# Key and value compression ahead of the query projections in the fill of the second block

## Chip, cores and metric

The kernel runs on one core of a Trainium2 chip. The metric is the device time of one execution in microseconds; the time before is the median of three runs. TensorE multiplies matrices and writes its results to PSUM; VectorE, ScalarE and GpSimd work on tiles in PSUM (not GpSimd) and SBUF; SP's queue issues most of the loads from device memory.

## What is computed

Two blocks over 512 tokens of width 1024, in 32-bit floats. The first block (two attentions, a gated merge, 32 experts of which four are used by each token) is not touched. The second block projects its input into 17 parts and feeds three mixers: a sparse attention (NSA, six heads in two groups), a stick-breaking attention (four heads) and a gated recurrence (HGRN, six heads). Their outputs are gated, projected and normalised. What the change touches belongs to the sparse attention:

```python
def compress(src, w1, w2):                     # for kc and vc
    blocks = src.reshape(B, S, G, dk)[:, blk_idx] + cmp_pos[None, None, :, None, :]
    blocks = blocks.transpose(0, 3, 1, 2, 4).reshape(B, G, n_cmp, CMP_BLOCK * dk)
    return jax.nn.gelu(blocks @ w1) @ w2

kc = compress(kc_src, w_ck1, w_ck2)
vc = compress(vc_src, w_cv1, w_cv2)
...
s_c = jnp.einsum('bghtd,bgnd->bghtn', qb, kc) * scale + bias_c
```

There are 31 overlapping blocks of 32 tokens; `w1` is 2048 x 128 and `w2` is 128 x 64. The scores of the queries against the compressed keys need both the compression and the query projections, and are computed well after either.

## The kernel before

The second block keeps its input transposed in SBUF, split into a high and a low half (`xTh`, `xTl`), so that a product in full precision is three matmuls: high by high, high by low, low by high (L132 to L134). A projection of 128 columns takes one chunk of weights (1024 x 128) and 24 matmuls, eight groups of three.

Weight chunks are loaded and split in the order of a list that `block2_plan` (L1191) writes; each chunk that is taken (`ws_get`, L211) writes the load of the second chunk after it and the split of the next one. A chunk is loaded by SP into `raw`, ScalarE copies the high half (L144) and VectorE subtracts it for the low half (L146). The chunks of the compression are kept as one tile of both halves (`whl`), those of the projections as two (`whi`, `wlo`). Buffers come from two pools: `S` with 17 large buffers (2048 elements per partition), `H` with 10 small ones (1024). A `raw`, a `whi` and a `wlo` of a 128-column chunk take a small one each, a `whl` a large one.

The order of the second block's work is written by hand. The recurrence (`hgrn`, L1609) runs in 66 steps, three head pairs through an input stage, a tree of six levels and an output stage. Beside it runs a fill: a chain of generators that give out matmuls piece by piece. `mix_in` (L64) takes 160 pieces of fill for 72 steps of the recurrence, and what is left of the fill behind them. The fill is the forget and query projections of the recurrence (`P_fq`, 32 pieces for the two that belong to the fill) and the parts that the string `F1` names, in its order:

- `s`, `P_stick` (L1324), 48 pieces: queries, keys and values of the stick-breaking attention
- `v`, `P_v` (L1344), 32: values, gates and two key projections of the sparse attention
- `p`, `P_blocks` (L1367), 16: the sources of the compression, laid out in overlapping blocks (`Y`)
- `b`, `block2_bias` (L1239), 1: the position biases, twelve matmuls (L1251), written to device memory and read back (`t5d`, `tz`)
- `q`, `P_nq` (L1436), 24: the three query projections; each result is split by ScalarE (L144) and VectorE (L148)
- `c`, `P_compress` (L1385), 16: for the key and then the value, sixteen matmuls of `Y` with the chunks of `w_ck1` or `w_cv1` (L1406), then the halves are summed by four matmuls (L1414), then gelu in small steps on VectorE and ScalarE (L1415 to L1421), then the product with `w2` (L1425 or L1431) and the layout of the result (L1427 to L1433); the key's result is split into `kc`

Behind the fill come the gated projections of the recurrence's output (`P_zh`, L1456) woven with the start of the stick-breaking attention, then that attention, the sparse attention (`nsa`, L1678) and the remaining gates, then the output projection.

The order of writing is a priority, not the order of the queues: at compile time a planner puts the instructions of each engine into its queue, and pulls later work ahead where earlier work isn't ready or has no buffer. On the chip each queue then runs in the order that was fixed.

Of the kernel before, what the change touches and what calls it, by code (L numbers as in the profile page):

```python
# [38 lines left out]
FI = -1  # L39
RP = 1  # L40
HP = 50
F1, F2, F3 = "svpbqc", "h", "z"
WS, WN, WZ = 34, 78, 50
NA, NB = 66, 38
ZO = 3, 0, 1, 4, 2
# [43 lines left out]
class K:  # L89
# [1101 lines left out]
    def block2_plan(self):  # L1191
        w, a = self.a["w_in_2"], self.a
        c0 = 0
        for n in [512] + [128] * 10 + [256, 128, 18] + [128] * 7 + ["w_ck1_2", "w_cv1_2"] + [128] * 8:
            if isinstance(n, str):
                for x in range(2):
                    self.ws_add([128, 8, 128], (lambda r: r, a[n][1024 * x:1024 * x + 1024].rearrange("(k p) c -> p k c", p=128)),
                                joint=True)
            else:
                if n == 512:  # L1200
                    self.ws_wide(w, c0)
                else:
                    self.ws_cols(w, c0, n)
                c0 += n
        w3 = a["w_out_2"].rearrange("(k p) c -> p k c", p=128)
        for x in (1, 0):
            for n in range(2):
                self.ws_add([128, 4, 512], (lambda r: r, w3[:, 4 * x:4 * x + 4, 512 * n:512 * n + 512]))
# [740 lines left out]
```

## Time and profile before

| | us |
|---|---|
| median of three runs | 2056.35 |
| lowest, highest run | 2055.72, 2062.5 |
| the profiled execution | 2060.52 |
| its span in the trace | 2058.7 |

The span runs from the first to the last instruction of the program; 1.8 us of the profiled execution lie around it. The second block's part that matters lies between 1690 and 1860 us of the span: the recurrence with its fill up to about 1848, then the gated projections and the attentions. In the rows below, an engine's busy time in a stretch is to be held against the stretch's length, and "idle before" in brackets is the time for which an engine stood still ahead of an instruction, with what ended it.

### The profile page before, as it was taken

The numbers are of one execution on the slowest core, as the hardware profiler recorded it, in microseconds if no ns is written. First come the engines' busy times: TensorE is split into PE (matmuls) and PEld (weight loads), VectorE is DVE, ScalarE is ACT, GpSimd is POOL, SyncE is SP. The second block draws the span as 40 slices with busy tenths as digits, with TensorE's granted clock in tenths as the row PEclk, the third lists the DMA queues.
The fourth block names the chain that finished last, engine by engine and source line by source line (L and its number), as shares of the span: only waits on it lengthen the run. The fifth ranks groups of instructions, "written<-read, shape, count | busy, mean of one in ns | idle before, by whom it ended". The sixth has DMA issues, their size and how long they took to land. (4 is left out here: it accounts for less than half of the span.)

```text
span 2058.7 us, 26167 instructions
## 1 busy us (share of the span) xinstructions
PE 1971.5 (96%) x9926; PEld 1592.3 (77%) x9926; DVE 1641.5 (80%) x2095; ACT 1242.7 (60%) x1342; POOL 353.8 (17%) x225
## 2 busy tenths in 40 slices
PE   5999999999999999999999799899998899999997
PEld 4777778878888888888888688688886678867765
DVE  5574444689999999999999798799998868557676
ACT  4564443347776768677776576676866456346651
POOL 3000000121223222222222222222221000010000
PEclk9999999999999999999999899999999999999998
DMA  6151214569999999999999799899998532141121
GB/s 196 53 169 44 72 61 145 208 251 341 374 365 368 377 376 373 375 370 377 364 382 367 296 371 356 312 373 369 380 372 325 214 101 71 35 131 42 58 105 41
DMA packets 162708, 512.71 MB, mean 249 GB/s; under 512 B 19913, under 2 KB 94953, under 8 KB 113424
## 3 DMA queue, kind: packets, MB, share of 16 engines
q1 hardware_dynamic: 139104, 466.80, 61.4%
q0 software_dynamic: 14448, 29.03, 3.9%
q10 hardware_dynamic: 9024, 15.16, 2.1%
q8 instruction: 79, 1.29, 0.2%
q14 instruction: 53, 0.43, 0.1%
HBM read 505.51 MB, written 28.97 MB: 260 GB/s over the span
## 5 line engine op out<-in xcount | busy, mean ns | idle before, releaser
L146 DVE TENSOR_TENSOR wlo<-raw,whi 128x2048 fp32r<-128x2048 f32 (+1 forms) x466 | 978.8, 2130 | 116.0 <-ACT whi L144 74.7
L144 ACT ACTIVATE whi<-raw 128x2048 fp32r<-128x2048 f32 (+1 forms) x466 | 819.6, 1792 | 193.3 <-PE sc L134 78.4
L133 PE MATMUL mm<-wlo,xT 128*128 128x512 f32 x1024 | 401.1, 392 | 8.8 <-DVE wlo L146 8.8
L134 PE MATMUL mm<-whi,xT 128*128 128x512 f32 x1024 | 405.6, 396 | 0.0
L132 PE MATMUL mm<-whi,xT 128*128 128x512 f32 x1024 | 360.0, 400 | 5.2 <-ACT whi L144 5.2
L959 POOL DMA_INDIRECT accd<-h,sx x30 | 158.1, 5271 | 466.4 <-DVE h L958 447.9
L133 PEld LDWEIGHTS mm<-wlo,xT 128*128 128x128 f32 x1024 | 193.6, 189 | 47.5 <-DVE wlo L146 9.8
L132 PEld LDWEIGHTS mm<-whi,xT 128*128 128x128 f32 x1024 | 193.7, 189 | 42.2 <-ACT whi L144 5.8
L134 PEld LDWEIGHTS mm<-whi,xT 128*128 128x128 f32 x1024 | 193.0, 188 | 39.4
L133 PE MATMUL sc<-wlo,xT 128*128 128x512 f32 x512 | 201.3, 393 | 0.0
L134 PE MATMUL sc<-whi,xT 128*128 128x512 f32 x512 | 200.6, 392 | 0.0
L132 PE MATMUL sc<-whi,xT 128*128 128x512 f32 x512 | 183.0, 391 | 0.0
L144 ACT ACTIVATE xT<-tp 128x512 fp32r<-128x512 f32 x126 | 74.9, 594 | 175.8 <-PE tp L898 174.1
L133 PEld LDWEIGHTS sc<-wlo,xT 128*128 128x128 f32 x512 | 96.8, 189 | 21.3 <-DVE wlo L146 0.6
L134 PEld LDWEIGHTS sc<-whi,xT 128*128 128x128 f32 x512 | 96.7, 189 | 20.6
L132 PEld LDWEIGHTS sc<-whi,xT 128*128 128x128 f32 x512 | 96.6, 189 | 20.3
L132 PE MATMUL mm<-hTh,whi 128*128 128x512 f32 x256 | 106.6, 416 | 0.3 <-ACT whi L144 0.3
L1167 ACT ACTIVATE p<-s,mn 128x128 f32<-128x128 f32 (+3 forms) x112 | 62.2, 557 | 73.2 <-DVE mn L1163 69.4
L1163 DVE CUSTOM_DVE_ANT_0 s<-sc,bias 128x256 f32<-128x256 f32 (+3 forms) x99 | 45.6, 482 | 74.2 <-PE sc L140 64.4
L874 POOL DMA_INDIRECT xg<-h1d,sx x31 | 74.0, 2386 | 168.6 <-PE mm L134 90.7
L134 PE MATMUL mm<-hTh,wlo 128*128 128x512 f32 x256 | 100.6, 393 | 0.6 <-DVE wlo L146 0.6
L133 PE MATMUL mm<-hTl,whi 128*128 128x512 f32 x256 | 100.8, 394 | 0.0
(463 smaller groups left out, 3091.4 us busy)
## 6 DMA issues: line engine op xcount, KB each, us to landing
raw<-in_w_exp_in_dram SPq DMA_DIRECT2D x256, 1024.0 KB, 7.4
raw<-in_w_exp_out_dram SPq DMA_DIRECT2D x128, 1024.0 KB, 7.3
raw<-in_w_in_dram SPq DMA_DIRECT2D x58, 512.0 KB, 3.9
raw<-in_w_out_dram SPq DMA_DIRECT2D x8, 1024.0 KB, 5.9
raw<-in_w_in_dram SPq DMA_DIRECT2D x7, 1024.0 KB, 8.4
x<-in_x_dram SPq DMA_DIRECT2D x4, 512.0 KB, 6.8
hd<-h SPq DMA_DIRECT2D x4, 512.0 KB, 2.6
raw<-in_w_branch_a_dram SPq DMA_DIRECT2D x4, 512.0 KB, 3.4
```

Of the source, the lines that this page charges most:

```text
L132: mm(out, lh, rh, start=start, stop=False, **kw)
L133: mm(out, lh, rl, start=False, stop=False, **kw)
L134: return mm(out, ll, rh, start=False, stop=stop, **kw)
L144: h = nc.scalar.activation(hi, src, AF.Copy, scale=scale)
L146: l = (eng or nc.vector).tensor_tensor(lo, src, f(hi), op=OP.subtract)
L874: self.nc.gpsimd.indirect_dma_start(out=dst, out_offset=None, in_=src[:, :], in_offset=bass.IndirectOffsetOnAxis(ap=ix[:, 0:1], axis=0), b ...
L959: nc.gpsimd.indirect_dma_start(out=self.accd[:, :], out_offset=bass.IndirectOffsetOnAxis(ap=ix[:, 0:1], axis=0), in_=y, in_offset=None, bo ...
L1163: nc.vector.tensor_tensor_reduce(s[:, :kl], sc[:, :kl], bias, op0=OP.add, op1=OP.min, scale=1.0, scalar=3e38, accum_out=mn)
L1167: nc.scalar.activation(p[:, :kl], s[:, :kl], AF.Exp, scale=-1.0, bias=mn, accum_out=sm)
```

## The change

The string `F1` names the compression ahead of the query projections, and the list of weight chunks puts the four chunks of the compression (two of `w_ck1`, two of `w_cv1`) ahead of the three of the queries, so that the list still agrees with the order in which chunks are taken. No instruction is added or removed.

```diff
-F1, F2, F3 = "svpbqc", "h", "z"
+F1, F2, F3 = "svpbcq", "h", "z"
...
     def block2_plan(self):
         w, a = self.a["w_in_2"], self.a
         c0 = 0
-        for n in [512] + [128] * 10 + [256, 128, 18] + [128] * 7 + ["w_ck1_2", "w_cv1_2"] + [128] * 8:
+        for n in [512] + [128] * 10 + [256, 128, 18] + [128] * 4 + ["w_ck1_2", "w_cv1_2"] + [128] * 11:
             if isinstance(n, str):
```

## Rows read from the trace of the kernel before

**Rows 1.** The profile's page, its first part: busy time, share of the span, instructions.

```profile
span 2058.7 us, 26167 instructions
...
PE 1971.5 (96%) x9926; PEld 1592.3 (77%) x9926; DVE 1641.5 (80%) x2095; ACT 1242.7 (60%) x1342; POOL 353.8 (17%) x225
```

**Rows 2.** Table by stretch: length, busy (instructions) per engine, clock, DMA share, GB/s.

```profile
1805.00:1830.50 25.50, 25.50 (x117) 18.41 (x116) 13.70 (x27) 13.27 (x21) 8.16 (x24) 1.00 0.58 176
1830.50:1842.70 12.20, 7.68 (x48) 7.03 (x47) 8.16 (x18) 5.27 (x8) 0.00 (x0) 0.72 0.58 144
1842.70:1860.00 17.30, 17.30 (x76) 11.98 (x75) 8.84 (x21) 10.51 (x17) 0.00 (x0) 1.00 0.11 30
1860.00:1900.00 40.00, 40.00 (x278) 31.95 (x276) 30.22 (x77) 20.54 (x37) 0.00 (x0) 1.00 0.15 41
1900.00:2020.00 120.00, 117.39 (x772) 82.25 (x772) 77.75 (x255) 68.67 (x158) 1.40 (x3) 1.00 0.21 70
```

**Rows 3.** Timeline of TensorE around the compression: start, us, line, tiles, idle before.

```profile
1829.68 0.39 PE L134 MATMUL mm<-xTh,wlo 128*128 128x512 f32 x1
...
1830.36 0.39 PE L134 MATMUL mm<-xTh,wlo 128*128 128x512 f32 x1
1830.59 2.08 PE L1406 MATMUL sc<-whl,Y 128*128 128x256 f32 x16
...
1835.62 0.43 PE L1425 MATMUL sc<-cw 128*128 128x64 f32 x2 [1.39 <-DVE cw L1421]
1839.16 3.75 PE L1406 MATMUL sc<-whl,Y 128*128 128x256 f32 x16 [3.10 <-DVE whl L146]
1842.74 0.40 PE L132 MATMUL mm<-xTh,whi 128*128 128x512 f32 x1
```

**Rows 4.** Timeline of ScalarE, same columns: splits of the compression's weights.

```profile
1821.25 1.05 ACT L144 ACTIVATE whl<-raw 128x1024 fp32r<-128x1024 f32 x1
...
1836.65 0.26 ACT L144 ACTIVATE kc<-cw 128x64 fp32r<-128x64 f32 x1 [1.56 <-DVE cw L1427]
1836.81 1.99 ACT L144 ACTIVATE whl<-raw 128x1024 fp32r<-128x1024 f32 x2
```

**Rows 5.** Table by stretch, finer, for the granted clock.

```profile
1835.60:1839.10 3.50, 0.43 (x2) 0.30 (x2) 1.82 (x5) 2.45 (x4) 0.00 (x0) 0.55 0.29 73
1839.10:1842.70 3.60, 3.54 (x16) 3.54 (x17) 3.41 (x4) 1.59 (x2) 0.00 (x0) 0.50 0.02 5
```

**Rows 6.** Timeline of SP's queue, 1800 to 1830: start, us, line, loads.

```profile
1805.10 8.76 SPq L194 DMA_DIRECT2D raw<-in_w_ck_dram  x2
1819.76 1.29 SPq L1712 DMA_DIRECT2D bias<-t5d  x3
...
1826.08 1.01 SPq L194 DMA_DIRECT2D raw<-in_w_cv_dram  x2
```

**Rows 7.** Timelines of ScalarE and VectorE: split of the first query chunk.

```profile
1799.47 1.06 ACT L144 ACTIVATE whi<-raw 128x1024 fp32r<-128x1024 f32 x1
...
1800.56 1.23 DVE L146 TENSOR_TENSOR wlo<-raw,whi 128x1024 fp32r<-128x1024 f32 x1 [1.80 <-ACT whi L144]
```

**Rows 8.** TensorE's groups, 1805 to 1848.2: busy us, mean ns, idle before.

```profile
L1251 PE MATMUL sc<-t,tb 32*128 32x384 f32 x12 | 4.9, 516 | 0.0
L1590 PE MATMUL mm<-hv,hs 128*128 128x64 f32 x16 | 2.2, 261 | 0.0
L1587 PE MATMUL mm<-hS,hw 128*128 128x128 f32 x6 | 1.2, 286 | 0.0
L1414 PE MATMUL sc<-cw 128*128 128x64 f32 x8 | 1.2, 274 | 0.0
L1585 PE MATMUL sc<-hv,p 128*128 128x128 f32 x6 | 1.1, 287 | 0.0
```

**Rows 9.** DMA issues, 1780 to 1860: count, KB each, us to landing.

```profile
raw<-in_w_in_dram SPq DMA_DIRECT2D x6, 512.0 KB, 5.2
raw<-in_w_ck_dram SPq DMA_DIRECT2D x2, 512.0 KB, 4.4
```

## The prediction

> **What bounds the kernel now.** I read four views, coarse to fine. The page comes first [rows 1]: TensorE is busy for 96% of a span of 2058.7 us, so only a stretch in which it stands still, or runs slowly, can give time back. The table by stretch of the second block comes next [rows 2]. The reader is to see that TensorE is full in every stretch from 1805 to 1900 but one: between 1830.5 and 1842.7 it is busy for 7.68 of 12.20 us, and its mean granted clock there is 0.72, against 1.00 before and after. The timeline of TensorE in that stretch [rows 3] shows what runs: the compression of keys and values. The last of the query projections ends at 1830.4; sixteen matmuls of the key compression take 2.08 us; then TensorE waits 1.39 us for VectorE's small steps on the compressed key and 3.10 us for the split of the value weights; then sixteen equal matmuls take 3.75 us. The two waits are 1.39 + 3.10 = 4.49 us, and the table agrees: 12.20 - 7.68 = 4.52.
>
> The timeline of ScalarE [rows 4] says why the second wait ends so late. ScalarE splits the first two value chunks only at 1836.81, right behind the small split of the compressed key, which itself waited 1.56 us for VectorE. So the stall is a chain of small steps with nothing else left for TensorE to do: the fill that ran beside the recurrent mixer is used up, and the next projections' weights stand behind the value weights.
>
> The clock is the other part. [...] The same work costs 3.75 - 2.08 = 1.67 us more there [rows 3]. Together 4.49 + 1.67 = **6.16 us** is what the compression loses by standing last.
>
> [...]
>
> **The change part by part.** No instruction is added or removed. The planner that orders the queues at compile time takes ready work by the order of writing, so the order string moves the work and the weight list moves the loads with it. The mixer has 66 steps and pulls 160/72 pieces of fill per step, 147 in all; of the 169 pieces, 129 lie ahead of the exchanged parts. Before, 18 of the 24 query pieces lie beside the mixer, and 6 query pieces and all 16 of the compression behind it. After, all 16 of the compression and 2 of the queries lie beside it, and 22 query pieces behind.
>
> Removed from the end of the fill: the two waits and the slow matmuls, if query work stands behind the compression. A query chunk is 24 matmuls, three of which take 1830.36 - 1829.68 = 0.68 us [rows 3], so 8 x 0.68 = 5.4 us a chunk and 16.3 us for three. That is more than twice the 6.2 us to be covered. The small steps of the compressed value then lie under queries, and the next projections' weights can be split under them too. Gain: up to 6.16 us.
>
> Moved on the queues: the four loads of compression weights go ahead of three query loads on SP, and with them the four small loads of the second compression weights. SP's issues take about 0.4 us each, and the line of waits on that queue is what counts: between 1805.10 and 1826.08 it passes two loads, then three bias loads, then the rest [rows 6]. On ScalarE and VectorE four splits go ahead of three query splits; both engines have room (13.27 and 13.70 us busy of 25.50 [rows 2]). On GpSimd two memsets move ahead, and stand before the reciprocal root of the last mixer group if they have to wait for their buffer; that root releases the output of the mixer, for which the next gated projections wait. I cost these at nothing: TensorE's projections hide them. If that cover is gone, the split of one chunk shows, 1.06 + 1.23 = 2.3 us [rows 7].
>
> Added at the front: at 1805 the first query chunk stands ready, with its weights split at 1799.47 and 1800.56 [rows 7]. Now the compression stands there, with little work per chunk: 2.08 / 2 = 1.04 us, against 2.3 us of split. The trace of before doesn't show that order, so this is bounded from both sides. Below: 0; no gain below zero, since TensorE is busy for 25.50 of 25.50 us there [rows 2]. Above: the late queries of the first rival, 9 us. I take 2.3 - 1.04 = 1.26, one split that a compression chunk doesn't cover, because the mixer and the bias matmuls (12 of them, 4.9 us [rows 8]) fill the rest; the nearest row is that of the split.
>
> Sum: 6.16 - 1.26 = **4.9 us**. Behind it TensorE is full up to 1900 [rows 2], so the gain should pass to the end. The profiled execution took 2060.52 us (2058.7 of span and 1.8 around it), 4.2 above the median of 2056.35; 2060.52 - 4.9 = 2055.6 there, and 2056.35 - 4.9 = **2051.4** at the median.
>
> **The rivals.**
>
> *Late query weights (slower).* Place: SP and the buffers. If the first query load is placed behind the three bias loads, it leaves at 1819.76 + 1.29 = 1821.1 [rows 6], lands 5.2 us later [rows 9] and is split 2.3 us after that, at 1828.6. From 1805 to then TensorE has the compression at the full clock (4.2 us), the bias matmuls (4.9), the mixer's output matmuls (2.2 + 1.2 + 1.1) and the compression's small products (1.2) [rows 3, 8], 14.8 of 23.6 us: 8.8 us of waiting. That is 8.8 - 6.16 = 2.6 us lost, and up to 1.67 more when the clock falls: 4 us, 2060.4 at the median. It decides where the first query load leaves later than 1805 + 14.8 + 6.16 - 7.5 = 1818.5. For it: in the run before, the loads that now stand in these places of the list left late as well: two within 8.76 us of 1805.10, and the next only at 1826.08, behind the bias loads [rows 6]. Against it: a compression chunk holds one small buffer until it is split and puts its halves into a large one, where a query chunk needs three small ones, so the loads behind it should find buffers earlier.
>
> *The change doesn't do what it says.* The compression's split halves take large buffers, of which there are 17. In the run before, the first key chunk was loaded at 1805.10 and landed in 4.4 us [rows 6, 9], but was split at 1821.25 [rows 4], 11.7 us later. If it was a large buffer that it waited for, the exchange in the program moves little on the engines: the compression still comes at about 1821, queries or not. Then TensorE waits at either place, and a gain of 0 to 3 us is left, 1.5 in the middle: 2054.9 at the median. [...]
>
> *More than the stall.* Buffers of the compression come free some 10 us earlier, and the stick-breaking scores start sooner. TensorE's idle time from 1900 to 2020 is 120 - 117.39 = 2.6 us [rows 2]; if that goes too, the gain is 8.8 us: 2047.6. Against it: those waits have owners of their own.
>
> **How the numbers follow.** Forecast, 3 to 6.2 us gained: 0.45. Late queries: 0.20. Little moved: 0.23. More than the stall: 0.12. The range takes the forecast, little moved and, nearly whole, the other two: 2046.5 to 2061. A measurement of this kernel tells about 0.3% from no change, 6.2 us, just the whole of the stall. Faster by more: the last rival and the upper edge of the forecast, 0.12 + 0.13 = 0.25. Slower by more: the part of the first rival in which a second and third query chunk are late as well, 0.11. Within: 0.64.
>
> **What would show it.** Right: in the profile after, the sixteen matmuls of the value compression follow within a few us of those of the key and take about 2.1 us; no wait over 1 us on the split compression weights; the query projections run as one dense stretch up to the gated projections; the low clock near 1840 is gone. The front is right if waits between 1800 and 1825 sum to about 1.3 us. Late queries would show as a wait of TensorE on a query weight and a query load behind the bias loads on SP. Little moved would show as query matmuls ahead of the compression's. The prediction is wrong if the gated projections start later than now (1842.74 [rows 3]), or if they start 5 us earlier and the end doesn't follow.

## The result, and the profile after

The changed kernel takes 2082.0 us at the median (2073.6 to 2086.5) beside 2057.6 for the kernel before on the same chip: a ratio of 1.0106, with a 95% interval of 1.0088 to 1.0123. That is some 22 us slower where 4.9 us faster was forecast, and far outside the range.

The profiled execution took 2086.48 us, 26.0 more than the one of before. The page of the changed kernel answers [rows 1]: the same number of instructions, 10 us more of busy TensorE, a smaller share.

```profile
span 2084.7 us, 26167 instructions
...
PE 1981.5 (95%) x9926; PEld 1598.9 (77%) x9926; DVE 1641.9 (79%) x2095; ACT 1242.8 (60%) x1342; POOL 358.8 (17%) x225
```

To see where, I cut both traces at two places that the change does not touch: the last matmul of the recurrence's tree (L1548) and the first of the second product of the stick-breaking (L1658). Up to the first cut the changed kernel is 3.4 us late (1807.8 against 1804.4; in e1, e2, e5 and e8 below, which have the same order up to there, it lay at 1799.6 to 1805.5, so this is one execution against another). Behind the second cut it is 1.0 us longer. The 21.6 us lie in between. The table by stretch, of before and then of after, from cut to cut (length, busy time of TensorE with its instructions, the weight loads, VectorE, ScalarE, GpSimd, granted clock, DMA share, GB/s):

```profile
1804.40:1866.50 62.10, 57.58 (x269) 42.92 (x269) 34.89 (x70) 34.98 (x51) 8.76 (x24) 0.95 0.42 117
```

```profile
1807.80:1891.50 83.70, 66.87 (x262) 48.88 (x262) 35.24 (x71) 35.95 (x52) 7.40 (x24) 0.78 0.29 82
...
1808.40:1833.90 25.50, 17.52 (x53) 10.86 (x52) 8.59 (x19) 9.89 (x16) 3.60 (x15) 0.57 0.40 123
1833.90:1846.10 12.20, 6.87 (x31) 6.68 (x32) 4.23 (x14) 1.83 (x4) 1.56 (x8) 0.50 0.29 76
1846.10:1856.90 10.80, 7.29 (x28) 4.79 (x28) 4.86 (x12) 3.96 (x6) 1.64 (x1) 0.84 0.19 49
1856.90:1875.00 18.10, 18.10 (x80) 13.91 (x81) 7.66 (x11) 4.72 (x7) 0.00 (x0) 1.00 0.23 59
```

TensorE stands still for 83.70 - 66.87 = 16.8 us (before 62.10 - 57.58 = 4.5) and is busy 9.3 us longer with nearly the same work (262 matmuls recorded where there were 269). So 12.3 us are waits and 9.3 us a slower clock. Cut into single microseconds from 1804 to 1892, the trace shows a granted clock of 1.00 in 48 of them, of 0.50 in 37 and a value between in three; so the mean of 0.78 over 83.7 us is an estimated 0.22 x 83.7 / 0.5 = 36.8 us at the lower level, 0.50, against some 6 us before (0.05 x 62.1 / 0.5). The first of the finer stretches answers the first line of [rows 2]: 25.50 of 25.50 us busy there has become 17.52, at a clock of 0.57.

The timeline of TensorE in the changed kernel (start, us, line, tiles, count, idle before and who ended it), which answers [rows 3]:

```profile
1808.08 0.40 PE L134 MATMUL mm<-xTh,wlo 128*128 128x512 f32 x1
1810.33 0.66 PE L1590 MATMUL mm<-hv,hs 128*128 128x64 f32 x4 [1.85 <-DVE hs L1550]
1810.92 2.03 PE L1251 MATMUL sc<-t,tb 32*128 32x384 f32 x4
1815.66 1.64 PE L1251 MATMUL sc<-t,tb 32*128 32x384 f32 x2 [2.71 <-ACT vec L1253]
...
1823.75 2.08 PE L1406 MATMUL sc<-whl,Y 128*128 128x256 f32 x8
...
1829.56 2.08 PE L1406 MATMUL sc<-whl,Y 128*128 128x256 f32 x8 [1.15 <-DVE whl L146]
1837.39 1.11 PE L1414 MATMUL sc<-cw 128*128 128x64 f32 x4 [5.76 <-ACT cw L1411]
1840.35 0.69 PE L1425 MATMUL sc<-cw 128*128 128x64 f32 x2 [1.84 <-DVE cw L1421]
...
1848.84 0.50 PE L132 MATMUL mm<-xTh,whi 128*128 128x512 f32 x1 [0.30 <-ACT whi L144]
...
1852.51 0.56 PE L134 MATMUL mm<-xTh,wlo 128*128 128x512 f32 x1 [2.23 <-DVE wlo L146]
```

The reader is to see that no projection matmul (L132 to L134) runs from 1808.5 to 1848.8. Before, the query projections stood here: their last matmul ended 26 us behind the tree ([rows 3]). What is left is small: bias matmuls, the mixer's output, the compression, each waiting for a small step of another engine. Eight compression matmuls take 2.08 us here, at a granted clock of 0.50 (1823.75 to 1825.60), which is what sixteen took before at 1.00 (1830.59 to 1832.60) [rows 3].

The timeline of ScalarE in the same kernel says why the query weights come so late (it answers [rows 4] and [rows 7]):

```profile
1823.86 0.49 ACT L1253 ACTIVATE vec<-sc 128x384 f32<-128x384 f32 x1 [2.56 <-PE sc L1251]
...
1827.19 2.00 ACT L144 ACTIVATE whl<-raw 128x1024 fp32r<-128x1024 f32 x2 [2.37 <-DMA t5d<-vec]
1836.02 1.06 ACT L144 ACTIVATE whl<-raw 128x1024 fp32r<-128x1024 f32 x1 [6.83 <-POOL t2c L1264]
1836.98 0.35 ACT L1411 COPY cw<-sc 128x256 f32<-128x256 f32 x1
1839.55 0.26 ACT L1419 ACTIVATE cw<-cw 128x64 f32<-128x64 f32 x1 [2.21 <-DVE cw L1418]
1841.50 0.26 ACT L144 ACTIVATE kc<-cw 128x64 fp32r<-128x64 f32 x1 [1.69 <-DVE cw L1427]
1846.97 0.60 ACT L1600 ACTIVATE p<-mm 128x512 f32<-128x512 f32 x1 [5.21 <-PE mm L1590]
1847.46 0.37 ACT L1411 COPY cw<-sc 128x256 f32<-128x256 f32 x1
1847.71 2.02 ACT L144 ACTIVATE whi<-raw 128x1024 fp32r<-128x1024 f32 x2
```

The first two query splits (whi, 1847.71) stand in ScalarE's queue behind the compression's splits, its chain of small steps and the mixer's output (L1600). Two of the compression's splits wait 2.37 and 6.83 us for large buffers that the biases' tables hold (vec until its rows are written out, tz until GpSimd has copied from it). SP's queue, which answers [rows 6]:

```profile
1802.11 3.55 SPq L194 DMA_DIRECT2D raw<-in_w_cv_dram  x2
1826.76 1.29 SPq L1712 DMA_DIRECT2D bias<-t5d  x3
1828.09 29.21 SPq L194 DMA_DIRECT2D raw<-in_w_in_dram  x5
```

The first query load does leave behind the three bias loads, as the first rival had it. Three causes therefore offered themselves: SP's order, the large buffers, and the order of the splits on ScalarE.

### The profile page after: what moved, and what is told of

The parts are those of the page before. It is cut to its first block, busy times and chain, and to the rows that moved or that the text cites. A ratio compares the mean times of both kernels' runs of the same rounds, so it can differ in the third digit from the quotient of the medians.

```text
span 2084.7 us, 26167 instructions
## 1 busy us (share of the span) xinstructions
PE 1981.5 (95%) x9926; PEld 1598.9 (77%) x9926; DVE 1641.9 (79%) x2095; ACT 1242.8 (60%) x1342; POOL 358.8 (17%) x225
## 5 line engine op out<-in xcount | busy, mean ns | idle before, releaser
L133 PE MATMUL mm<-wlo,xT 128*128 128x512 f32 x1024 | 401.4, 392 | 11.2 <-DVE wlo L146 11.1
L134 PE MATMUL mm<-whi,xT 128*128 128x512 f32 x1024 | 406.0, 397 | 0.0
L132 PE MATMUL mm<-whi,xT 128*128 128x512 f32 x1024 | 360.2, 400 | 5.1 <-ACT whi L144 5.1
L132 PEld LDWEIGHTS mm<-whi,xT 128*128 128x128 f32 x1024 | 193.8, 190 | 42.2 <-ACT whi L144 5.7
L134 PEld LDWEIGHTS mm<-whi,xT 128*128 128x128 f32 x1024 | 193.2, 189 | 39.5
L134 PE MATMUL sc<-whi,xT 128*128 128x512 f32 x512 | 200.5, 392 | 0.0
L132 PE MATMUL sc<-whi,xT 128*128 128x512 f32 x512 | 182.5, 390 | 0.0
L134 PEld LDWEIGHTS sc<-whi,xT 128*128 128x128 f32 x512 | 96.4, 188 | 20.5
L132 PEld LDWEIGHTS sc<-whi,xT 128*128 128x128 f32 x512 | 96.4, 188 | 20.2
L132 PE MATMUL mm<-hTh,whi 128*128 128x512 f32 x256 | 106.6, 416 | 0.7 <-ACT whi L144 0.7
L1167 ACT ACTIVATE p<-s,mn 128x128 f32<-128x128 f32 (+3 forms) x112 | 62.2, 557 | 73.6 <-DVE mn L1163 69.7
L134 PE MATMUL mm<-hTh,wlo 128*128 128x512 f32 x256 | 100.6, 393 | 0.6 <-DVE wlo L146 0.6
L874 POOL DMA_INDIRECT h<-accd,sx x30 | 58.0, 1933 | 249.8 <-ACT whi L144 75.1
```

The source lines that it names most:

```text
L132: mm(out, lh, rh, start=start, stop=False, **kw)
L133: mm(out, lh, rl, start=False, stop=False, **kw)
L134: return mm(out, ll, rh, start=False, stop=stop, **kw)
L874: self.nc.gpsimd.indirect_dma_start(out=dst, out_offset=None, in_=src[:, :], in_offset=bass.IndirectOffsetOnAxis(ap=ix[:, 0:1], axis=0), b ...
L1167: nc.scalar.activation(p[:, :kl], s[:, :kl], AF.Exp, scale=-1.0, bias=mn, accum_out=sm)
```

## The experiments

Each run stands beside runs of the kernel before on the same chip. Stretch, idle time of TensorE and granted clock are of the profiled execution, cut as above; idle is the length less the busy time. The first cut lies between 1797.3 (e7) and 1807.8 us (after), and in every run the last projection of `P_blocks` ends 0.7 us behind it, so the stretches can be compared.

| kernel | median us | ratio to before (95%) | stretch us | idle us | clock |
|---|---|---|---|---|---|
| before | 2057.6 | | 62.1 | 4.5 | 0.95 |
| after | 2082.0 | 1.0106 (1.0088 to 1.0123) | 83.7 | 16.8 | 0.78 |
| e1, bias loads off SP | 2079.6 | 1.0103 (1.0076 to 1.0130) | 83.3 | 16.7 | 0.80 |
| e2, one large buffer free | 2078.6 | 1.0096 (1.0070 to 1.0122) | 80.9 | 14.7 | 0.79 |
| e3, compression ahead of the biases | 2070.7 | 1.0060 (1.0041 to 1.0080) | 72.8 | 9.3 | 0.84 |
| e4, queries around the compression | 2067.8 | 1.0038 (1.0018 to 1.0058) | 71.5 | 7.6 | 0.83 |
| e5, both large buffers free | 2079.6 | 1.0098 (1.0075 to 1.0121) | 81.3 | 17.1 | 0.83 |
| e6, look-ahead of 3 | 2064.1 | 1.0024 (1.0009 to 1.0038) | 66.5 | 5.5 | 0.87 |
| e7, e3 and look-ahead of 3 | 2068.3 | 1.0045 (1.0029 to 1.0061) | 68.9 | 6.9 | 0.85 |
| e8, 64 spare matmuls | 2083.1 | 1.0109 (1.0086 to 1.0133) | 82.8 | 10.9 | 0.84 |
| e9, two queries first | 2069.4 | 1.0029 (1.0012 to 1.0045) | 72.3 | 10.4 | 0.83 |
| e10, e9 and look-ahead of 3 | 2061.9 | 1.0003 (0.9988 to 1.0018) | 65.2 | 5.3 | 0.95 |
| e11, look-ahead of 4 | 2064.1 | 1.0009 (0.9990 to 1.0027) | 66.3 | 6.7 | 0.87 |
| e12, look-ahead of 3, both buffers | 2072.9 | 1.0044 (1.0024 to 1.0064) | 76.3 | 15.8 | 0.82 |
| e13, both buffers, bias loads off SP | 2076.1 | 1.0072 (1.0054 to 1.0090) | 77.6 | 13.2 | 0.82 |
| e14, look-ahead of 3, bias loads off SP | 2064.4 | 1.0019 (1.0007 to 1.0032) | 64.8 | 5.2 | 0.89 |
| e15, e12 and bias loads off SP | 2074.6 | 1.0067 (1.0048 to 1.0085) | 76.1 | 15.7 | 0.82 |
| e16, e10 and both buffers, loads off SP | 2070.3 | 1.0044 (1.0027 to 1.0062) | 73.6 | 11.1 | 0.84 |
| e17, one query first, look-ahead of 3, loads off SP | 2065.1 | 1.0020 (1.0002 to 1.0039) | 67.1 | 9.4 | 0.90 |
| e18, e10 and bias loads off SP | 2060.4 | 1.0006 (0.9988 to 1.0023) | 64.8 | 5.0 | 0.95 |

The before beside e9 to e16 had a median of 2060.3 to 2060.5, beside the others 2057.6 to 2058.7; so the ratio is the column to compare, not the microseconds.

**SP's order (e1).**

```diff
-                    nc.sync.dma_start(bias[:, 256:512], bass.AP(tensor=d.tensor, offset=d.offset + 384 * h + 127,
+                    nc.gpsimd.dma_start(bias[:, 256:512], bass.AP(tensor=d.tensor, offset=d.offset + 384 * h + 127,
```

> The kernel after, with the sparse attention's bias loads (L1712) issued by GpSimd instead of SP, so that the three query loads no longer stand behind them on SP; nothing else. Theory Q (the queue: the late query weights come from SP's order): query loads leave some 15 to 20 us earlier, query matmuls fill the waits from 1810 to 1857, 15 to 22 us of the 24 us lost come back, about 2060. Theory B (the buffers: the splits of the compression's weights wait for the large buffers that the biases hold, and all else is queued behind them): the loads may leave earlier, but find no small buffer or wait on ScalarE behind the same splits; at most 5 us come back, about 2078.

The loads moved and the splits did not. In e1 the timeline of SP has the first query load 1.5 us behind the tree's end (which is at 1799.6 here), where the changed kernel had it 20.3 us behind it:

```profile
1801.08 37.15 SPq L194 DMA_DIRECT2D raw<-in_w_in_dram  x4
```

and the timeline of ScalarE still has the query splits 39.4 us behind the tree's end (after: 39.9), in the same queue:

```profile
1827.26 1.06 ACT L144 ACTIVATE whl<-raw 128x1024 fp32r<-128x1024 f32 x1 [6.29 <-POOL t2c L1264]
...
1838.27 0.60 ACT L1600 ACTIVATE p<-mm 128x512 f32<-128x512 f32 x1 [5.28 <-PE mm L1590]
1838.76 0.37 ACT L1411 COPY cw<-sc 128x256 f32<-128x256 f32 x1
1839.02 2.01 ACT L144 ACTIVATE whi<-raw 128x1024 fp32r<-128x1024 f32 x2
```

A load that is 19 us early is worth nothing when its split stands where it stood. SP's order as the sole cause is refuted.

**Large buffers (e2, e5).** In e2 vec goes to the work buffers of the mixer's p tiles (the diff down to the line with `self.w`); e5 also cuts tz into two small buffers, each with a load of its own.

```diff
-        vec = self.slot([128, 4, 384], F32, "vec")
...
-            v = vec[:, h % 4, :]
+            v = self.w([128, 512], F32, "p", 4)[:, :384]
...
-        tz = self.slot([128, 6, 256], F32, "tz")
+        tz = [self.slot([128, 3, 256], F32, "tz") for _ in range(2)]
```

> The kernel after, with the six rows of position biases on their way to device memory (vec) in four rotating buffers that the kernel has anyway, instead of in one of the 17 large ones; SP's order is that of the kernel after. Theory B: the second split of the key weights doesn't wait for vec (it began at 1827.2), the key compression ends some 10 us earlier, 8 to 15 us come back, about 2070. Theory Q: the query loads still leave behind the bias loads, at about 1828, TensorE has nothing to do until then, and at most 4 us come back, about 2079.

> The changed kernel, with both of the biases' tables out of the large buffers: the four rows of vec go to the work buffers that the mixer's p tiles use, and tz to two small buffers. No split of the compression can wait for a table of the biases any more; the place of every part in the order string stays. Before 2058.3 us, after 2082.0, 21.7 us of it between the recurrence's tree and the second product of the stick-breaking. Theory B (large buffers hold the compression's splits): ScalarE's waits ahead of those splits (6.83 and 2.37 us in the profile of the changed kernel) and TensorE's wait of 5.76 us go, the compression is done some 9 us earlier, and at least 10 us come back: about 2070. Theory S (what is short is TensorE's work: the query weights' splits are written into ScalarE's queue behind the compression's chain and the mixer's output, because the look-ahead of the weight stream counts chunks and a compression chunk holds 1.04 us of TensorE's work): the 5.76 us wait goes, but the waits move on to the next thing, the query splits come only a few us earlier, and 3 to 7 us come back: 2075 to 2079.

In e2 ScalarE's long wait falls from 6.83 to 4.57 us and 2.8 us of the stretch come back, not the 8 to 15 of the theory of the buffers; so neither theory holds by itself: SP's order failed in e1, the one large buffer here. In e5 both waits for buffers are gone, and the scheduler, free to, sets the bias loads ahead of the value weights' loads on SP. ScalarE in e5 waits for those weights instead:

```profile
1826.08 1.06 ACT L144 ACTIVATE whl<-raw 128x1024 fp32r<-128x1024 f32 x1 [5.44 <-DMA raw<-in_w_cv_dram]
```

The 10 us that the buffers alone would have given back are not there; the wait changed its owner and hardly its size. That left open whether buffers and SP's order hide each other, so e13 takes both away.

> The changed kernel with both: the biases' tables out of the large buffers (e5) and the bias loads on GpSimd's queue and not on SP (e1). Nothing of the biases is in front of a compression load or split any more. Two halves of one cause: the waits of 6.83 us (buffer) and 5.44 us (load) go together, the compression is done by +20 us of the recurrence's tree, and 8 to 14 us come back: 2068 to 2074. Split order alone: the query splits still stand behind the compression's chain and the second half of the mixer's output on ScalarE, the first query is evicted no earlier than +40 us, and no more than 3 to 7 us come back: 2075 to 2079.

e13 is still 1.0072 times the kernel before, and its first query projection is evicted only 46 us behind the tree's end. About 7 us come back by the ratio (1.0106 to 1.0072), at the upper edge of what the split order alone allowed. Buffers and SP's order together are a smaller part.

**Compression ahead of the biases (e3), queries around it (e4).** e3 changes the string to "svpcbq"; e4 takes one query, the key compression, a query, the value compression, a query, with the list in that order.

> The compression ahead of the position biases too (order string svpcbq, the weight list of the kernel after). The compression's splits come ahead of the biases' large buffers, and the planner puts the query loads ahead of the bias loads on SP. Both theories expect the loss to go; Q and B together 20 us or more, about 2060 or, if the stall of before is hidden as forecast, 2053. If it stays above 2075, neither is the cause, and the compression standing beside the recurrence with little work for TensorE is itself the cost.

> One query projection, the key compression, one query projection, the value compression, the last query projection; weight list in that order. If the compression needs query work on both sides, ready beside it, this hides the stall of the kernel before without starving the recurrence: 3 to 6 us faster than before, about 2052. If the last query load, which the planner again puts behind the bias loads on SP, is what counts (theory Q), one chunk of 5.4 us is late: 2058 to 2064. Theory B alone: waits on the splits remain as in the kernel before, about 2057.

By the ratios e3 gives back some 9 and e4 14 of the 22 us, both less than was expected of them. e4 still loses 8 us, its third query evicted 50.8 us behind the tree's end. In e3 no split waits for a buffer, and 11 us of the stretch come back. What remains is the same queue: the query splits of e3 stand behind L1600 and L1411 again, on ScalarE:

```profile
1823.24 0.60 ACT L1600 ACTIVATE p<-mm 128x512 f32<-128x512 f32 x1 [3.32 <-PE mm L1590]
...
1823.74 0.37 ACT L1411 COPY cw<-sc 128x256 f32<-128x256 f32 x1
1823.99 2.02 ACT L144 ACTIVATE whi<-raw 128x1024 fp32r<-128x1024 f32 x2
```

**The order of the splits (e6, e7, e11).** The weight stream splits one chunk ahead of the one in use (L2 = 1, 1). The fourth compression chunk is the one whose use writes the first query split, and it is used late. e6 leaves the order of the parts as it is in the changed kernel and raises only that number, with the loads that go along:

```diff
         def P_compress():
             Ys = T["Y"]
+            self.look_l, self.look_s = 1, 3
...
             for j in range(3):
                 yield from proj_t()
+                self.look_l, self.look_s = L2
```

> The changed kernel, with the look-ahead of the weight stream raised from one split chunk to three from the start of the compression to the end of the first query projection. Loads and splits of the query weights are thereby written ahead of the compression's last chunks, and ScalarE's queue has the first query split ahead of the three late compression splits. The order string and the work stay. Theory S (split order on ScalarE): the first query split comes about 15 us earlier than at 1847 and its 24 matmuls fill the waits of the compression; 8 to 14 us come back: 2068 to 2074, with idle time of TensorE between tree and second product down from 16.9 to about 8 us. Theory B (large buffers): the three late compression splits stand where they stood, behind tz, and nothing or at most 3 us comes back: 2079 to 2082.

> Compression ahead of the biases (as in e3, 2070.65 us, where no large buffer is held by the biases when the compression splits) and the look-ahead of three as in e6. In e3 the compression was done 18 us behind the tree, but the query splits stood on ScalarE behind the mixer's output at +24 us. Theory S: both query splits now stand ahead of that, the waits of 3.4 and 3.0 us go, and 6 to 11 us come back: 2060 to 2065. A theory that only the sum of loads and splits per chunk counts (ScalarE and VectorE are too slow for chunks with 1.04 us of matmuls, in whatever order): no more than 3 us come back: 2068 to 2071.

> The changed kernel with a look-ahead of four split chunks instead of the three of e6 (2064.1 us; the changed kernel 2082). ScalarE's queue then has two query splits ahead of the late compression splits and not one. Theory S: more of the same, 1 to 4 us under e6: 2060 to 2063. Theory B (what is left in e6 is ScalarE's wait of 4.39 us for the buffer tz, which holds the third late compression split): that wait stays, and nothing more comes back: 2063 to 2066.

e6 gives back 17 us of the 22 by the ratios (1.0106 to 1.0024), more than expected, in spite of the buffers and of SP's order; 5 us are left. ScalarE in e6 splits the first query chunk 11.9 us behind the tree's end (1802.8), ahead of tz and of three of the four compression splits:

```profile
1814.74 1.06 ACT L144 ACTIVATE whi<-raw 128x1024 fp32r<-128x1024 f32 x1 [0.21 <-issue]
...
1823.43 1.06 ACT L144 ACTIVATE whl<-raw 128x1024 fp32r<-128x1024 f32 x1 [4.39 <-POOL t2c L1264]
```

ScalarE's wait for tz's buffer is still 4.39 us long there, but nothing comes of it, because TensorE has a query projection in hand (its timeline in e6):

```profile
1816.93 0.53 PE L132 MATMUL mm<-xTh,whi 128*128 128x512 f32 x1
...
1822.32 0.39 PE L134 MATMUL mm<-xTh,wlo 128*128 128x512 f32 x1
1822.55 1.12 PE L1407 MATMUL sc<-whl,Y 128*128 128x256 f32 x8
```

What is left in e6 is mostly not waiting: TensorE is idle for 5.5 us (before: 4.5), but busy for 61.0 where it was 57.6. Its twelve bias matmuls, with no projection between them, take 7.57 us there, and 4.9 before [rows 8]:

```profile
1805.90 7.57 PE L1251 MATMUL sc<-t,tb 32*128 32x384 f32 x12
```

This is the run on which the verdict rests: the same order of the parts, the same buffers, the bias loads on SP, and only the splits (with their loads) written earlier; that earlier loads alone bring little is e1. A fourth chunk (e11) has the same median, and a ratio 0.0015 smaller with an interval that overlaps: the two are not told apart. e7 missed: 2 to 3 us under e3 where 6 to 11 were expected, and with intervals that overlap. Its time is the one that was named for the rival theory (only the sum of loads and splits counts, in whatever order); e6, which gains 17 us with the same loads and splits, speaks against that. In e7 the wait of 3.00 us went as expected, but the other, 3.41 us for the split of a key chunk 6.6 us behind the tree's end, stands as in e3: the compression is where nothing else is ready. The clock has a part too. Behind its first eight bias matmuls (1826.0 to 1829.1) TensorE works for ten us without a pause at a granted clock of 0.53; at 1.00 that would have taken an estimated 10 x 0.53 = 5.3 us, if the time of this work goes with the granted clock as that of the compression matmuls does in after and before (in 2.08 us eight at 0.50, sixteen at 1.00); table by stretch of e7:

```profile
1830.00:1840.00 10.00, 10.00 (x23) 6.31 (x22) 1.00 (x3) 1.70 (x4) 1.41 (x7) 0.53 0.43 133
```

**Is TensorE starved? (e8).** Ahead of each half of the compression, 32 spare matmuls on operands that are there; the first real one overwrites what they leave.

> The changed kernel with 32 spare matmuls (256 columns, on operands that are there) ahead of the key compression and 32 ahead of the value compression; the first real matmul overwrites what they leave. They cost 64 x 0.13 = 8.3 us at the full clock and twice that at the low level, if TensorE has no room. Starved TensorE (theories S and B alike): they go into the waits that are there, idle time falls by about as much as they take, and the time rises by 0 to 4 us: 2082 to 2086. Clock theory (the low level is a cause of its own and not only a companion of the waits): TensorE stands still less, the low level lasts shorter than the 37.5 us of the changed kernel, and the time falls by 2 to 6 us in spite of the added work: 2076 to 2080. TensorE not starved: the time rises by 8 us or more: 2090 or above.

TensorE's timeline in e8:

```profile
1821.42 6.40 PE L1408 MATMUL sc<-Y 128*128 128x256 f32 x32
1827.67 1.12 PE L1409 MATMUL sc<-whl,Y 128*128 128x256 f32 x8
...
1837.98 6.63 PE L1408 MATMUL sc<-Y 128*128 128x256 f32 x32
```

13.0 us of added work show no cost clear of the noise: the ratio goes from 1.0106 to 1.0109, inside both intervals, and the stretch from 83.7 to 82.8 us. Idle time falls from 16.8 to 10.9 us and the granted clock rises from 0.78 to 0.84; without the spare matmuls TensorE is busy for 82.8 - 10.9 - 13.0 = 58.9 us, where it was 66.9. So TensorE is starved, as expected. Whether the clock is a second cause this run does not tell: the 66.9 - 58.9 = 8 us that came back beside the higher clock were used up by the spare matmuls themselves. It is not a clean run either, since the planner set the first two query splits ahead of the mixer's output, 33.4 us behind the tree's end instead of 39.9.

**Queries ahead (e9, e10, e17, e18).** The list and the parts give two queries (e17: one), the compression, the rest; e10, e17 and e18 with the look-ahead of e6, e17 and e18 with the bias loads off SP.

```diff
+        def P_x():
+            q, c = P_nq(), P_compress()
+            for x in "qqkvq":
+                yield from some(q if x == "q" else c, 8)
...
```

> Two query projections, then the compression, then the third query projection, the weight list in that order; look-ahead of one split chunk as in the kernels before and after. Theory S (a query chunk whose split is written behind compression chunks comes too late, because the look-ahead counts chunks and the compression's hold little work): one query of the three stands behind the compression and is late, where the changed kernel has three (23 us lost) and e4, with queries between the two halves, lost 9 us; the two in front are evicted as early as before, and the third behind +45 us of the recurrence's tree. Time 2059 to 2066. If it were enough that query work stands behind the compression (the step on which the prediction rests): the stall of 6.2 us is covered, 2052 to 2056.

> As e9, with the look-ahead of three split chunks from the start of the compression on, so that the third query's split is written ahead of the compression's small steps. Theory S: the third query's matmuls run in the waits of the compression (1.39 and 3.10 us in the kernel before) and the low level goes with them; this is the gain that the change was forecast to bring: 2 to 6 us under the kernel before, 2052.5 to 2057, idle time of TensorE in the stretch under 3 us. A theory that the compression costs its waits in every order (its chain of small steps is the owner): 2058 to 2062.

> One query projection, the compression, two query projections; look-ahead of three split chunks from the start of the compression on, bias loads on GpSimd's queue. If work in hand for TensorE beside the biases and the mixer's output is what is short (theory S: e14, none in front, has 13.7 us of low clock and idle 5.3 us): one query in front fills the waits ahead of the biases, and two behind fill those of the compression: 2055 to 2060, equal to or under the kernel before. If the gain of the forecast (6.2 us for the compression's own waits) is there to be had at all, this order shows it best: under 2056. If not: as e10 and e14, 2061 to 2064.

> e10 (two queries, compression, third query, look-ahead of three; 2061.9 us beside 2060.5) with the bias loads on GpSimd's queue, the tables in the large buffers as before. If SP's order is part of what is left in e10 (three loads of query and gated projections left SP only at 1824.5, behind the bias loads at 1818.2): 2 to 4 us under e10, 2058 to 2060. If not: 2061 to 2063.

e9 loses 6 us by the ratio, and its largest wait is a lesson of its own. TensorE waits 5.14 us for the compressed key's small steps:

```profile
1838.44 0.69 PE L1425 MATMUL sc<-cw 128*128 128x64 f32 x2 [5.14 <-DVE cw L1421]
```

VectorE's timeline in e9 shows them (L1416, ready since 1833.6) standing behind a split and behind an operation of the mixer's output that waits for GpSimd:

```profile
1833.34 0.23 DVE L1415 COPY cw<-sc 128x64 f32<-128x64 f32 x1 [1.31 <-PE sc L1414]
...
1833.55 1.22 DVE L146 TENSOR_TENSOR whl<-raw,whl 128x1024 fp32r<-128x1024 f32 x1
1836.30 0.69 DVE L1605 TENSOR_TENSOR ho<-mm,hrs 128x512 f32<-128x512 f32 x1 [1.53 <-POOL hrs L1604]
1836.91 0.21 DVE L1416 TENSOR_TENSOR cw<-cw 128x64 f32<-128x64 f32 x1
```

Its third query is evicted 51.5 us behind the tree's end, as late as the first of the changed kernel (52.2): one query behind the compression comes as late as three. With the look-ahead (e10, e18) the loss is gone, 1.0003 and 1.0006 with intervals on both sides of 1. The 2 to 6 us of gain that e10 was expected to show are not there. In e10 the waits of the compression do shrink (1.52 and 1.07 us instead of 1.39 and 3.10), but a wait of 2.09 us shows in the stick-breaking, and the low clock, 0.51, now lies at 1808 to 1815. Two rows of the table by stretch of e10 show it with no wait ahead of it:

```profile
1798.90:1808.30 9.40, 9.40 (x38) 6.15 (x36) 5.92 (x13) 6.66 (x11) 3.16 (x10) 1.00 0.40 109
1808.30:1815.20 6.90, 6.90 (x14) 4.32 (x14) 1.00 (x3) 1.61 (x3) 1.32 (x6) 0.51 0.77 249
```

TensorE is busy without a pause on both sides; eight of the twelve bias matmuls stand in the first row, four in the second. At the 1.00 of the first row the second row's work would have taken an estimated 6.90 x 0.51 = 3.5 us, so 3.4 us go there. In the kernel before, with more projection matmuls between the bias matmuls, the clock beside them (1809.3 to 1816.8) was 1.00 [rows 2]. e18 is not told apart from e10, so SP's order is not what is left there. e17 is 4 us slower than the kernel before (1.0002 to 1.0039), above every range named for it.

**Both cures at once (e12, e14, e15, e16).**

> The changed kernel with both cures, the look-ahead of three of e6 (2064.1 us) and the biases' tables out of the large buffers of e5 (2079.6 us, 2.5 us under the changed kernel). If buffers are a second cause beside the split order: 2 to 5 us under e6, 2059 to 2062. If they are not, the same as e6 within 2 us, 2062 to 2066. ScalarE's queue has all but one query split behind the biases' small steps here, so a loss is possible too if those small steps wait.

> e6 (look-ahead of three, 2064.1 us) with the bias loads on GpSimd's queue. In e6 four query loads stood behind the bias loads until 1817.7. If SP's order is a second cause behind the split order: 2 to 4 us under e6, 2060 to 2062. If not: within 2 us of e6.

> e12 (look-ahead of three, tables out of the large buffers, 2072.9 us) with the bias loads on GpSimd's queue. e12 was 9 us slower than e6; in its profile TensorE waits 10.85 us for a chain that begins at ScalarE's wait of 6.72 us for a value weight's load behind the bias loads. If that load is the reason: the wait goes and 8 us or more come back, 2060 to 2065. If freeing the buffers is harmful for another reason: no more than 3 us come back, 2070 to 2073.

> e10 (two queries, compression, third query, look-ahead of three; 2061.9 us beside a before of 2060.5) with the tables out of the large buffers and the bias loads on GpSimd's queue. ScalarE's wait of 4.33 us for tz's buffer and TensorE's 1.52 us behind it go. Split order, buffers and SP's order as parts of one supply: 2 to 4 us under e10, 1 to 4 us under the kernel before, 2055 to 2059. If the chain of the compressed key is what is left (1.07 us) and the low level beside the bias matmuls (6.8 us): as e10, 2060 to 2063.

e14 equals e6: behind the look-ahead SP's order costs nothing. e12, e15 and e16 came out 4, 10 and 8 us slower by the ratios than the same kernels without the freed buffers (e6, e14, e18), each above every range named for it. For e12 the intervals overlap, but its stretch is 9.8 us longer than that of e6. On ScalarE in e12 an operation of the mixer, whose input VectorE had ready at 1822.3, stands behind a compression split whose weight is still on its way:

```profile
1827.55 1.06 ACT L144 ACTIVATE whl<-raw 128x1024 fp32r<-128x1024 f32 x1 [6.72 <-DMA raw<-in_w_cv_dram]
1828.52 0.61 ACT L1567 ACTIVATE hw<-hw 128x512 f32<-128x512 f32 x1
```

The timeline of TensorE in e12 has the longest wait of the run behind that:

```profile
1830.53 1.11 PE L1575 MATMUL tp<-ident,hw 128*128 128x128 f32 x4 [10.85 <-DVE hw L1568]
```

TensorE waits 10.85 us for what follows from it, which is the mixer's output and not fill. I had named the bias loads on SP as the reason and expected e15 to cure it; it did not. In e15 the small second weights (L1401) stood on SP for 27.6 us for the bias rows written from the mixer's buffers, and a wait of 4.47 us for the value weight was left. So moving a table out of one kind of buffer made others late; which part of the 4 to 10 us belongs to which of these was not separated.

## Why the prediction was wrong, point by point

**The step that failed** is in "Moved on the queues": four splits go ahead of three query splits on ScalarE and VectorE, "both engines have room", "I cost these at nothing". Room by busy share was not room in the queue. Both engines are less busy in the changed kernel (9.89 and 8.59 us of 25.50 where [rows 2] had 13.27 and 13.70), and yet the query splits come 45 us later with respect to the tree (from 4.9 us ahead of its end to 39.9 behind it). Ready work stood behind instructions that waited: in after, e1 and e12 on ScalarE behind waits of 5.2, 5.3 and 6.7 us, in e9 on VectorE behind one of 1.5 us. I knew the 2.3 us of one split and priced part of that; the price was the whole queue ahead of it. That it was this place in the queue, and not the loads or the buffers alone, is shown by e6: with the splits written earlier, and the order of the parts as in the changed kernel, 17 of the 22 us came back. The 5 us that were left lie mostly in slower matmuls (61.0 - 57.6 = 3.4 us of busy time in e6); no run took that away by itself.

**"Added at the front: 1.26 us"** fell with it. The assumption was that the mixer and the bias matmuls fill the rest. They wait themselves (1.85 and 2.71 us), and without a query projection beside them nothing covers that: 12.3 us of idle time and 9.3 us of slower work instead of 1.26. The sum had no term at all for a slower clock at the front, which was granted 0.57 in its first 25.5 us.

**The gain of 6.16 us** had the condition that query work stands behind the compression. It stood there in the order of writing, but not split. Where it was made ready (e10, e18) the 3.10 us wait did go, and the time still only reached that of the kernel before. So also the step "the gain should pass to the end" is not borne out. In e10's profile 2.09 us are a new wait in the stick-breaking and an estimated 3.4 us the granted clock of 0.51 beside the bias matmuls; no run took either away, so whether the gain is there to be had stays open.

**The clock.** The 1.67 us in the sum are the difference of two measured times, sixteen matmuls in 2.08 us at a granted clock of 1.00 and in 3.75 at 0.50 [rows 3, 5], and the kernel before was at 0.50 for some 6 us. The changed kernel was at 0.50 for some 37 us, and TensorE was busy 9.3 us longer than before. For part of that time it had nothing to run: from 1812 to 1846, at 0.50, it was idle for 34.0 - 22.5 = 11.5 us.

**The rivals.** "Late query weights" had the right sign and the right sight (a query load behind the bias loads), at 0.20, but the wrong mechanism, which e1 refuted, and 4 us instead of 22: it ended the lateness at the split of the first chunk and let the compression run at the full clock, where the key's sixteen matmuls ran at 0.50 (1823.75 to 1825.60, 1829.56 to 1831.60). "The change doesn't do what it says" was right that the compression does not come early (its last matmuls end 39 us behind the tree) and that large buffers hold its splits; it was wrong that TensorE loses nothing then. "More than the stall" did not occur.

**The signs I named.** The gated projections starting later than 1842.74 was the sign of a wrong prediction, and it came: the last query projection is evicted at 1870.65 us.

## What to carry to other kernels

Before moving a part ahead, list in each engine's queue what stands between the old and the new place of every instruction that feeds it, and add up what those instructions wait for: a busy share of one half said nothing about that here. A look-ahead that counts chunks shrinks when the chunks get smaller: four chunks of 1 us of matmuls in front of 5.4 us chunks cut the time ahead in which the next weights are split from an estimated five microseconds of matmuls to one, and raising the count gave 17 of the 22 us back without touching the order of the parts. When a wait is taken away, look first for the next owner: freed buffers turned into loads that left later, and cost 4 to 10 us.

## What the runs showed of the hardware that I had not expected

TensorE's clock fell without a wait: in e10 it was busy for all 16.3 us from 1798.9 to 1815.2, and the granted clock went from 1.00 to 0.51 at 1808.3, between the bias matmuls. 64 spare matmuls, 13.0 us of TensorE's time, showed no cost clear of the noise in the changed kernel (e8): they filled 5.9 us of waits, and the work beside them ran some 8 us faster, at a granted clock of 0.84 instead of 0.78. The compression matmuls, of 128 rows, took 2.08 us for eight at a granted clock of 0.50 (after) and for sixteen at 1.00 (before). The bias matmuls, of 32 rows, took longer at the lower clock too: in e10 four took 1.55 us in the row at 1.00 and 2.92 in the row at 0.51, and all twelve took 2.03 + 1.64 + 2.92 + 1.65 = 8.2 us in the changed kernel against 4.9 [rows 8].
